# Layer 0's mixture of experts: the loop of extra blocks before the last block's outputs

## The chip, the cores and the metric

The kernel runs on one core of one Trainium2 chip. The metric is the device time of one execution in microseconds (us), as a median over runs. One execution is also recorded by the hardware profiler; all rows below come from that one. Engines are named as the profile names them: PE is TensorE, DVE is VectorE, ACT is ScalarE, POOL is GpSimd, and SP issues most of the DMAs.

## The reference, cut to what matters

The reference is a two-layer backbone over 256 context and 256 latent tokens, 1024 channels wide. Each layer mixes tokens (three branches) and then runs a mixture of experts. The change lies at the end of layer 0's mixture of experts and at the start of layer 1:

```python
combine = sum(one_hot(e_idx, 16) * w[..., None], axis=1)   # the two chosen experts of each token
gate = einsum('nd,edf->nef', t, w_gate)
up   = einsum('nd,edf->nef', t, w_up)
act  = silu(gate) * up * combine[..., None]
y    = einsum('nef,efd->nd', act, w_down)
...
xc = xc + mod_c[5] * f[:, :n_ctx]      # gated residual of the context tokens
xl = xl + mod_l[5] * f[:, n_ctx:]      # and of the latent ones
# the next layer begins with
hc = modulate(rms_norm(xc, norm_mix[1]), mod_c[0], mod_c[1])
hl = modulate(rms_norm(xl, norm_mix[1]), mod_l[0], mod_l[1])
```

## The kernel before, in words

The 512 tokens lie in four tiles of 128, `x[0]` to `x[3]`; tiles 0 and 1 are context, 2 and 3 latent. Layer 0's 16 experts are sorted by the number of their tokens and computed in blocks of 128 token slots. A block holds one large expert (`b < 5`, products split into three exact parts on PE) or two small ones of 64 slots (`b` from 5 on, computed half by half). `ORDER` fixes the row of blocks; the last two are block 4 (large) and block 8 (its halves are experts 12 and 13).

For every entry of that row `moe0` runs `full_in` or `half_in` (gate and up products), in the midst of it turns the entry before (`mid`), then runs the output products of the entry before (`finish`, with `down` or `outputs`). The outputs of ten blocks are written to a staging tensor `yd` in HBM. Those of the blocks in `KEPT` (4 and 8) stay on the chip as pairs `y`, already multiplied by the gate (`gated`).

When the row of blocks is through, three things follow:

- the staged rows of each token's two experts are gathered from `yd` by eight indirect DMAs on POOL (two for each token tile), and `total(t)` weights, adds and gates them and adds the sum to `x[t]`;
- a loop over extra blocks (`For_i`, `n` read from a register) covers experts with more tokens than their slots. Every engine and every DMA is waited for where the loop begins. In this run `n` is 0: the body's instructions do not show in the trace;
- `scatter` multiplies the kept pairs by one-hot matrices (`ot`) into rows of tokens, and `put2` adds them to `x`. `norm_r` then squares and sums `x[t]`, and `next_h` turns each tile for layer 1: `dr` (a diagonal of the norm), eight products on PE (L481), `hf` (scale and shift, DVE and ACT by turns), `hh` (ACT) and `hl` (DVE or POOL). Layer 1's first projection (L153 to L155) reads `hh` and `hl`.

The order on an engine is the scheduler's, except where `in_order(engine)` ties the instructions to the order in which they are written; before, this holds for PE through the row of blocks. `issue_after` puts single operations behind a named instruction. SP loads the weights in written order; `load_ahead` issues layer 1's first ones (`wq` twice, `wkv`) ahead.

Names that the text below uses: gates `gate[b]` (L1706, L1707), `total` (L1725 to L1728), the loop (L1742), the outputs of block 8 (L1470), `scatter` (L1524, L1525), `put2` (L1579), the squares (L346), `rv` and `rr` (L162, L163), `dr` (L476), `hf` (L486 on ACT, L488 on DVE), `hh` (L491), `hl` (L492), the splits `wh`, `wl` of a weight (L172, L173).

## Time and profile before

| | us |
|---|---|
| median of 3 runs | 1539.14 (1538.92 to 1540.22) |
| profiled execution, its own time | 1538.08 |
| profiled execution, span from first to last instruction | 1536.0 |
| PE busy | 1416.1 (92%) |
| DVE busy | 932.9 (61%) |
| ACT busy | 669.9 (44%) |
| POOL busy | 116.2 (8%) |

PE is busy nearly everywhere; what it is not busy with stands in a few holes. The change concerns the stretch from about 885 to 970 us. Times are counted from the span's start.

### The profile page before, as it was taken

How to read it: one execution, taken by the hardware profiler on the slowest of the kernel's cores; microseconds unless marked ns; L12 is line 12 of the kernel's file. 1: busy time of each engine (PE TensorE's matmuls, PEld its weight loads, DVE VectorE, ACT ScalarE, POOL GpSimd, SP SyncE). 2: the span in 40 equal slices, each digit the busy share in tenths (PEclk: the TensorE clock that was granted, in tenths of full speed). 3: DMA queues.
4: the chain of work that ended last, by engine and by line, in shares of the span. 5: the costliest groups of instructions: out<-in, count | busy, mean ns of one | idle time of the engine just before them, and what ended most of it. 6: DMA issues, size and time to landing. Idle time of an engine off the chain costs nothing. (4 is left out here: it accounts for less than half of the span.)

```text
span 1536.0 us, 20642 instructions
## 1 busy us (share of the span) xinstructions
PE 1416.1 (92%) x7431; PEld 929.2 (60%) x7431; DVE 932.9 (61%) x2154; ACT 669.9 (44%) x1333; POOL 116.2 (8%) x127
## 2 busy tenths in 40 slices
PE   5989999999999998699999966899999997999996
PEld 3766665687675666565555635788788775333332
DVE  4575556866564278897554666757977786423322
ACT  3344445735343235364454624555775553211112
POOL 1110000010000003200000022300001000000000
PEclk9999999999999999899999987999999999999999
DMA  8535425421135884499999993332333268899994
GB/s 324 208 144 217 152 96 199 144 101 57 56 108 205 310 299 145 170 354 381 421 421 422 418 362 130 139 136 87 120 128 100 97 223 348 364 423 424 424 423 178
DMA packets 56777, 363.11 MB, mean 236 GB/s; under 512 B 6368, under 2 KB 6368, under 8 KB 18528
## 3 DMA queue, kind: packets, MB, share of 16 engines
q1 hardware_dynamic: 47376, 328.49, 54.7%
q0 software_dynamic: 6400, 23.08, 4.4%
q10 hardware_dynamic: 2896, 10.19, 1.7%
q8 instruction: 60, 0.98, 0.3%
q14 instruction: 45, 0.37, 0.1%
HBM read 350.19 MB, written 11.54 MB: 236 GB/s over the span
## 5 line engine op out<-in xcount | busy, mean ns | idle before, releaser
L173 DVE TENSOR_TENSOR wl<-w,wh 128x512 fp32r<-128x512 f32 (+2 forms) x456 | 311.1, 699 | 184.2 <-ACT wh L172 168.2
L172 ACT CAST wh<-w 128x512 fp32r<-128x512 f32 (+2 forms) x456 | 270.8, 607 | 259.7 <-PE acc L233 127.3
L232 PE MATMUL acc<-hh,wh 128*128 128x512 f32 (+1 forms) x528 | 183.9, 348 | 0.2 <-ACT wh L172 0.2
L234 PE MATMUL acc<-hh,wl 128*128 128x512 f32 (+1 forms) x528 | 179.9, 341 | 1.4 <-DVE wl L173 1.4
L233 PE MATMUL acc<-hl,wh 128*128 128x512 f32 (+1 forms) x528 | 180.6, 342 | 0.0
L1447 PE MATMUL at<-w,xT 128*64 128x512 f32 x512 | 122.0, 600 | 1.1 <-DVE act L1452 0.8
L232 PEld LDWEIGHTS acc<-hh,wh 128*128 128x128 f32 x528 | 100.1, 190 | 31.2 <-issue 10.8
L234 PEld LDWEIGHTS acc<-hh,wl 128*128 128x128 f32 x528 | 100.1, 190 | 14.6 <-DVE wl L173 3.1
L233 PEld LDWEIGHTS acc<-hl,wh 128*128 128x128 f32 x528 | 100.1, 190 | 11.9 <-issue 2.1
L154 PE MATMUL acc<-wl,hh 128*128 128x512 f32 (+3 forms) x256 | 90.5, 354 | 5.4 <-DVE wl L173 5.4
L153 PE MATMUL acc<-wh,hh 128*128 128x512 f32 (+3 forms) x256 | 90.4, 356 | 2.8 <-DVE rv L162 2.3
L155 PE MATMUL acc<-wh,hl 128*128 128x512 f32 (+3 forms) x256 | 88.8, 350 | 0.0
L515 ACT ACTIVATE p<-at,nm 128x512 f32<-128x512 f32 (+1 forms) x96 | 59.1, 617 | 45.7 <-DVE nm L514 45.2
L1447 PE MATMUL acc<-w,xT 128*64 128x512 f32 x320 | 76.7, 606 | 1.6 <-DMA w<-in_moeu_dram 1.6
L163 POOL TENSOR_TENSOR rr<-rv,mhalf 128x1 f32<-128x1 f32 (+2 forms) x41 | 33.3, 813 | 524.5 <-DVE rv L162 517.0
L1447 PEld LDWEIGHTS at<-w,xT 128*64 128x64 f32 x512 | 33.5, 136 | 59.5 <-issue 55.2
L514 DVE TENSOR_REDUCE nm<-at 128x1 f32<-128x512 f32 (+1 forms) x96 | 56.5, 594 | 12.5 <-PE at L628 7.7
L232 PE MATMUL acc<-oh,wh 128*128 128x512 f32 (+1 forms) x160 | 59.5, 373 | 0.0
L154 PEld LDWEIGHTS acc<-wl,hh 128*128 128x128 f32 x256 | 49.7, 194 | 11.8 <-DVE wl L173 7.6
L1470 PE MATMUL at<-w,aT 128*64 128x512 f32 x256 | 56.7, 595 | 0.0
L233 PE MATMUL acc<-ol,wh 128*128 128x512 f32 (+1 forms) x160 | 55.9, 350 | 0.0
L234 PE MATMUL acc<-oh,wl 128*128 128x512 f32 (+1 forms) x160 | 55.8, 349 | 0.0
(504 smaller groups left out, 2638.8 us busy)
## 6 DMA issues: line engine op xcount, KB each, us to landing
w<-in_moeg_dram SPq DMA_DIRECT2D x64, 1024.0 KB, 16.0
w<-in_moeu_dram SPq DMA_DIRECT2D x64, 1024.0 KB, 17.9
w<-in_moed_dram SPq DMA_DIRECT2D x64, 1024.0 KB, 18.9
w<-in_wmod_dram SPq DMA_DIRECT2D x48, 1024.0 KB, 5.3
w<-in_wg_dram SPq DMA_DIRECT2D x24, 1024.0 KB, 4.8
w<-in_wb_dram SPq DMA_DIRECT2D x12, 1024.0 KB, 4.7
w<-in_wout_dram SPq DMA_DIRECT2D x8, 1024.0 KB, 7.1
w<-in_wx_dram SPq DMA_DIRECT2D x4, 1024.0 KB, 5.0
```

The lines of the kernel that those rows point to most:

```text
L153: nc.tensor.matmul(acc, ah, bh, start=start, stop=False)
L154: nc.tensor.matmul(acc, ah, bl, start=False, stop=False)
L155: nc.tensor.matmul(acc, al, bh, start=False, stop=stop)
L172: nc.scalar.copy(h, src)
L173: nc.vector.tensor_sub(l, src, h.bitcast(F32))
L232: nc.tensor.matmul(a[:, :n], h[:, i, :], hh[:, k, t0:], start=k == 0, stop=False)
L233: nc.tensor.matmul(a[:, :n], h[:, i, :], hl[:, k, t0:], start=False, stop=False)
L234: nc.tensor.matmul(a[:, :n], l[:, i, :], hh[:, k, t0:], start=False, stop=k == kc - 1)
L514: nc.vector.tensor_reduce(nm, sc[h][:, :nk], axis=AX.X, op=OP.max, negate=True)
L515: nc.scalar.activation(p[:, :nk], sc[h][:, :nk], AF.Exp, bias=nm, accum_out=sm)
L1447: nc.tensor.matmul(a[i * 64:i * 64 + 64], xT[:, k], ws[i][k // 4][:, k % 4], start=k == 0, stop=k == 7, tile_position=(0, i * 64))
L1470: self.nc.tensor.matmul(ya[n][64 * j:64 * j + 64], aT[:, k, 64 * j:64 * j + 64], w[k // 2][:, k % 2, n * 512:(n + 1) * 512], start=k == 0, ...
```

## The change

The loop of extra blocks now stands ahead of the turn and the output products of block 8's second half. The gathers of tiles 2 and 3 go into the buffers of the inputs `xh` and `xl`, and are issued when block 4's outputs begin; those of tiles 0 and 1 go into weight buffers, after the last weight loads. `total(2)` and `total(3)` precede the loop, `total(0)` runs beside the last outputs, and `total(1)`, wholly on DVE, in the midst of `scatter`. `scatter` goes through all four tiles of one half of the channels, then of the other; the squares are taken by halves. After the loop, until layer 1's tokens are turned, PE and DVE each follow the written order. The gates are computed one block earlier. Inside the loop's body buffers change too; the body isn't run here.

```diff
     def load_ahead(self, *loads):
-        ready = [self.load(*a) for a in loads]
-        self.ready.extend(ready)
+        ready, self.ready = self.ready, ()
+        loaded = [self.load(*a) for a in loads]
+        self.ready = collections.deque([*ready, *loaded])
...
-        for t in (2, 3, 0, 1):
-            for n in range(2):
+        for n in range(2):
+            for t in (2, 3, 0, 1):
                 a = bank()
...
             def put2(t, n, a):
                 c = x[t][:, n * 512:(n + 1) * 512]
-                ins = nc.vector.tensor_add(c, c, a)
-                if (t, n) == (3, 1):
-                    for i in (0, 1):
-                        total(i, (self.last, ins))
+                nc.vector.tensor_add(c, c, a)
+                if n == 0:
+                    sq[t] = self.small.tile([128, 2], F32, name="ssq")
+                    if t == 1:
+                        total(1)
+                if t == 1:
+                    if n:
+                        self.norms[t] = self.norm_r(x[t], junk)
+                    return
+                nc.scalar.activation(junk[:, :512], c, AF.Square, accum_out=sq[t][:, n:n + 1])
                 if n:
-                    self.norms[t] = self.norm_r(x[t], junk)
+                    ss = self.small.tile([128, 1], F32, name="ss")
+                    nc.vector.tensor_add(ss, sq[t][:, 0:1], sq[t][:, 1:2])
+                    self.norms[t] = self.rstd(ss, 1, D)
...
+            def rows(t, y):
+                ys[t] = y
+                for i in range(2):
+                    nc.gpsimd.indirect_dma_start(out=y[i], out_offset=None, in_=self.yd,
+                                                 in_offset=bass.IndirectOffsetOnAxis(ap=rt["row"][:, i, t:t + 1], axis=0))
+            def total(t):
+                y1, y2 = ys[t]
+                nc.scalar.activation(y1, y1, AF.Copy, scale=rt["w1"][:, t])
+                nc.vector.scalar_tensor_tensor(y1, y2, rt["w2"][:, t], y1, op0=OP.mult, op1=OP.add)
+                nc.vector.tensor_tensor(y1, y1, g2[t // 2], op=OP.mult)
+                nc.vector.tensor_tensor(x[t], x[t], y1, op=OP.add)
...
-                    with self.tc.issue_after(self.made[1].ins):
+                    with self.tc.issue_after(cut.ins):
                         for i, q in enumerate(KEPT):
...
+                    for t in (2, 3):
+                        rows(t, [T.tile([128, 8, 128], F32R, name=s).bitcast(F32).rearrange("p k q -> p (k q)")
+                                 for s in ("xh", "xl")])
                 if before:
                     finish(*before[:3])
+                    cut = self.cut
...
+            for t in (0, 1):
+                w = w2.tile([128, WG], F32, name="w")
+                rows(t, [w[:, i * D:(i + 1) * D] for i in range(2)])
-            turn(*before[:2], before[3])
             for t in (2, 3):
-                total(t, (self.made[0], self.made[-1]))
-            finish(*before[:3])
+                with self.tc.issue_after(gated[0].ins), self.tc.issue_after(gated[1].ins):
+                    total(t)
             order.close()
-            ot = T2.tile([128, 8, 128], F32R, name="xT", bufs=1)
-            last = [y + (self.spread(ot[:, 4 * i:4 * i + 4], rt["tok"][:, i]),) for i, y in enumerate(kept)]
-            self.load_ahead(*((self.I["wq"][1, i], 4) for i in range(2)), (self.I["wkv"][1], 8))
+            self.load_ahead(*((self.I["wq"][1, i], 4) for i in range(2)))
...
             with self.tc.For_i(0, n, 1) as i:
...
+            self.order = ExitStack()
+            for g in (mybir.EngineType.PE, mybir.EngineType.DVE):
+                self.order.enter_context(self.in_order(g))
+            turn(*before[:2], before[3])
+            ot = T2.tile([128, 8, 128], F32R, name="xT", bufs=1)
             junk = T2.tile([128, D], F32, name="yg", bufs=1)
-            self.feed(0, self.scatter(last, put2, self.acc))
+            spread = [self.spread(ot[:, 4 * i:4 * i + 4], rt["tok"][:, i]) for i in range(2)]
+            total(0)
+            finish(*before[:3])
+            self.load_ahead((self.I["wkv"][1], 8))
+            self.feed(0, self.scatter([y + (s,) for y, s in zip(kept, spread)], put2, self.acc))
             self.drain()
...
                     self.next_h(T, x[t], t, 1, hh, hl)
+            self.order.close()
             return mix, hh, hl, pre
```

In the rows of instructions below, line numbers after the change are the changed kernel's own. PE at the loop, before: `w,xT` are block 8's gate and up products, `tp<-cp,act` its turn, `w,aT` its outputs, and the compare and branch is the loop's beginning.

```order
L1447 MATMUL acc<-w,xT 64x512 x8
L1460 MATMUL tp<-cp,act 128x64 x4
L1470 MATMUL acc<-w,aT 64x512 x16
L1741 TENSOR_LOAD rctl
L1742 COMPARE_AND_BRANCH
```

PE where it leaves the loop, after the change (`yh,xT` and so on are `scatter`'s products):

```order
L1756 COMPARE_AND_BRANCH
L1756 UNCONDITIONAL_BRANCH
L1463 MATMUL tp<-cp,act 128x64 x4
L1473 MATMUL acc<-w,aT 64x512 x16
L1527 MATMUL acc<-yh,xT 128x512
L1528 MATMUL acc<-yl,xT 128x512
```

The second turn and the sixteen output products moved from ahead of the loop to behind it.

DVE between `scatter`'s sums and the first `dr`, before (numbers are those of the buffers; `x2`, `x3`, `x0`, `x1` are the token tiles):

```order
L1579 TENSOR_TENSOR x2_4997<-x2_4997,acc_8585 128x512
L1579 TENSOR_TENSOR x3_4998<-x3_4998,acc_8597 128x512
L1579 TENSOR_TENSOR x3_4998<-x3_4998,acc_8603 128x512
L162 TENSOR_SCALAR rv_8593<-ss_8591 128x1
L173 TENSOR_TENSOR wl_8729<-w_8219,wh_8728 128x512
L173 TENSOR_TENSOR wl_8733<-w_8219,wh_8732 128x512
L1726 SCALAR_TENSOR_TENSOR w_8169<-w_8169,rw2_5014 128x1024
L1726 SCALAR_TENSOR_TENSOR w_8172<-w_8172,rw2_5014 128x1024
L1727 TENSOR_TENSOR w_8169<-w_8169,xg_8021 128x1024
L162 TENSOR_SCALAR rv_8619<-ss_8617 128x1
L476 TENSOR_SCALAR dr_8673<-cp_72,rr_8594 128x128
```

The same after the change, from the first tile's second half on:

```order
L1585 TENSOR_TENSOR x2_4997<-x2_4997,acc_8619 128x512
L1598 TENSOR_TENSOR ss_8626<-ssq_8590 128x1
L163 TENSOR_SCALAR rv_8628<-ss_8626 128x1
L1585 TENSOR_TENSOR x3_4998<-x3_4998,acc_8632 128x512
L1598 TENSOR_TENSOR ss_8639<-ssq_8598 128x1
L163 TENSOR_SCALAR rv_8641<-ss_8639 128x1
L1585 TENSOR_TENSOR x0_4995<-x0_4995,acc_8645 128x512
L1598 TENSOR_TENSOR ss_8652<-ssq_8606 128x1
L163 TENSOR_SCALAR rv_8654<-ss_8652 128x1
L1585 TENSOR_TENSOR x1_4996<-x1_4996,acc_8658 128x512
L163 TENSOR_SCALAR rv_8666<-ss_8664 128x1
L477 TENSOR_SCALAR dr_8684<-cp_72,rr_8629 128x128
```

The first `dr` moved behind the sums and norms of all four tiles, and each `ss` reads squares of its own tile that ACT takes in between.

DVE from the turn of the first tile to that of the third after the change (`hf`, `hl` of tile 2, then `dr`, `hf`, `hl` of tile 3, then the splits `wl` of layer 1's first weights); before, both `dr` and all of these splits stood ahead of the first `hl`:

```order
L489 TENSOR_SCALAR hf_8686<-tp_8696,modA1_2512,modB1_2513 128x128
L493 TENSOR_TENSOR hl_8679<-hf_8686,hh_8678 128x8x128
L477 TENSOR_SCALAR dr_8708<-cp_72,rr_8642 128x128
L489 TENSOR_SCALAR hf_8710<-tp_8711,modA1_2512,modB1_2513 128x128 x2
L489 TENSOR_SCALAR hf_8710<-tp_8720,modA1_2512,modB1_2513 128x128 x2
L493 TENSOR_TENSOR hl_8679<-hf_8710,hh_8678 128x8x128
L174 TENSOR_TENSOR wl_8732<-w_8185,wh_8731 128x512
L174 TENSOR_TENSOR wl_8736<-w_8185,wh_8735 128x512
```

The second tile's `dr` moved behind the first tile's `hl`, and the splits behind the second tile's.

## Rows read from the trace of the kernel before

**Rows 1.** Stretches by their busy time; columns in the first row.
```profile
core 0: us, PE busy (x) PEld busy (x) DVE busy (x) ACT busy (x) POOL busy (x), PEclk, DMA share, GB/s
885.90:908.50 22.60, 18.10 (x77) 8.76 (x77) 12.35 (x23) 4.99 (x8) 4.39 (x4) 0.92 1.01 419
925.90:935.40 9.50, 9.48 (x32) 7.31 (x32) 7.03 (x11) 5.94 (x10) 0.95 (x1) 0.79 0.67 231
951.20:967.30 16.10, 16.07 (x83) 13.54 (x83) 11.60 (x29) 11.02 (x22) 3.27 (x2) 0.92 0.07 19
```
**Rows 2.** Timeline at the loop: start, us, engine, line, instruction, [idle before, releaser].
```profile
903.98 0.43 PE L1460 MATMUL tp<-cp,act 64*128 64x64 f32 x4 [1.61 <-DVE act L1452]
904.34 7.81 PE L1470 MATMUL acc<-w,aT 128*64 128x512 f32 x32
...
917.95 0.94 POOL L1718 DMA_INDIRECT w<-yd,rrow  x1 [0.30 <-issue]
925.87 0.80 PE L1524 MATMUL acc<-yh,xT 128*128 128x512 f32 x1 [13.72 <-issue]
```
**Rows 3.** The gather issued at 917.95 alone, and SP's waits, 905 to 930.
```profile
DMA to landing us min/median/max: 6.4/6.4/6.4
...
SPq L1742 <- DMA w<-yd,rrow: 10.7, 2, 8.4
```
**Rows 4.** DMA queues, 885.9 to 924.4: packets, MB, share of 16 engines.
```profile
q1 hardware_dynamic: 1247, 9.01, 57.6%
q0 software_dynamic: 1152, 4.19, 29.3%
```
**Rows 5.** The same, 904 to 906, gathers beside weight loads.
```profile
q0 software_dynamic: 125, 0.48, 59.9%
q1 hardware_dynamic: 48, 0.35, 42.4%
```
**Rows 6.** PE's wait behind the gates of the kept blocks.
```profile
892.60 0.80 PE L154 MATMUL acc<-wl,ah 128*128 128x512 f32 x1 [2.89 <-DVE wl L173]
```
**Rows 7.** Timeline from the first tile's norm to layer 1's first product.
```profile
936.15 3.25 POOL L1727 TENSOR_TENSOR w<-w,xg 128x1024 f32<-128x1024 f32 x1 [2.64 <-DVE w L1726]
937.19 2.30 DVE L476 TENSOR_SCALAR dr<-cp,rr 128x128 f32<-128x128 f32 x1
939.54 3.23 PE L481 MATMUL tp<-dr,x 128*128 128x128 f32 x16 [4.15 <-DVE dr L476]
951.21 0.77 PE L153 MATMUL acc<-wh,hh 128*128 128x512 f32 x1
```
**Rows 8.** Groups by shape, 905 to 919.6: count | busy us, mean ns.
```profile
L1726 DVE SCALAR_TENSOR_TENSOR w<-w,rw 128x1024 f32<-128x1024 f32 x2 | 2.6, 1280 | 4.3 <-ACT w L1725 4.3
L1507 DVE SCALAR_TENSOR_TENSOR act<-acc,rws,w 128x512 f32<-128x512 f32 x2 | 1.4, 742 | 0.0
```
**Rows 9.** Groups by shape, 939.5 to 957.
```profile
L488 DVE TENSOR_SCALAR hf<-tp,modA,modB 128x128 f32<-128x128 f32 x11 | 4.2, 404 | 3.1 <-PE tp L481 2.6 <-ACT hf L486 0.5
L486 ACT ACTIVATE hf<-tp,modB,modA 128x128 f32<-128x128 f32 x9 | 3.9, 451 | 2.8 <-DVE hf L488 2.8
L1579 DVE TENSOR_TENSOR x<-x,acc 128x512 f32<-128x512 f32 x4 | 2.5, 682 | 2.2 <-POOL x L1728 2.2
L492 DVE TENSOR_TENSOR hl<-hf,hh 128x1024 fp32r<-128x1024 f32 x2 | 2.4, 1216 | 0.0
L346 ACT ACTIVATE yg<-x 128x1024 f32<-128x1024 f32 x2 | 2.1, 1049 | 10.2 <-DVE x L1579 10.2
L491 ACT CAST hh<-hf 128x1024 fp32r<-128x1024 f32 x2 | 2.1, 1044 | 0.1
L476 DVE TENSOR_SCALAR dr<-cp,rr 128x128 f32<-128x128 f32 x3 | 0.8, 279 | 0.1
```

**Rows 10.** The page's costliest groups: the split's cast and difference (512 columns).
```profile
L173 DVE TENSOR_TENSOR wl<-w,wh 128x512 fp32r<-128x512 f32 (+2 forms) x456 | 311.1, 699 | 184.2 <-ACT wh L172 168.2
L172 ACT CAST wh<-w 128x512 fp32r<-128x512 f32 (+2 forms) x456 | 270.8, 607 | 259.7 <-PE acc L233 127.3
```

More of the change, by code (lines that the diff above doesn't have):

```diff
@@ L172, in split @@
         nc.scalar.copy(h, src)
-        nc.vector.tensor_sub(l, src, h.bitcast(F32))
+        self.cut = nc.vector.tensor_sub(l, src, h.bitcast(F32))
         return h, l
@@ L1385, in full_turned, with full_in @@
         return xh, xl
-    def full_in(self, T, x, ws, acc, mid=None, late=None):
+    def full_in(self, T, x, ws, acc, mid=None, late=None, act=None):
         nc = self.nc
@@ L1399, in full_in @@
                 self.fill()
-        act = T.tile([128, 512], F32, name="act", bufs=3)
+        if act is None:
+            act = T.tile([128, 512], F32, name="act", bufs=3)
         nc.scalar.activation(act, ga, AF.Silu)
@@ L1569, in pair, with middle @@
                 return tuple(T.tile([128, 2, 512], F32R, name=n, bufs=b) for n, b in (h, l))
+            def middle():
+                return T.tile([128, 4, 128], F32R, name="ot", bufs=1).bitcast(F32).rearrange("p k q -> p (k q)")
             def put1(t, n, a):
                 c = slice(n * 512, (n + 1) * 512)
-                z = T.tile([128, 512], F32, name="act", bufs=3)
+                z = middle()
                 nc.vector.tensor_mul(z, a, g2[t // 2][:, c])
@@ L1591, in out @@
                     i = len(kept)
-                    if i:
-                        w = wa.tile([128, WG], F32, name="w").bitcast(F32R).rearrange("p (a n c) -> p a n c", a=2, n=2)
-                        y = w[:, 0], w[:, 1]
-                    else:
-                        y = pair(("yh", 1), ("yl", 1))
+                    y = pair(("xh", 2), ("xl", 2)) if i else pair(("yh", 1), ("yl", 1))
                     kept.append(y)
@@ L1668, in finish @@
                 out(self.down(T, mids[b], downs[p], self.acc) if b < 5 else
-                    self.outputs(mids[b], [downs[q] for q in MADE[b]], self.acc), b)
+                    self.outputs(mids[b], [downs[q] for q in MADE[b]], self.acc, b in KEPT), b)
+            def rows(t, y):
[9 more added lines that the diff above has]
+                nc.vector.tensor_tensor(x[t], x[t], y1, op=OP.add)
+            ys, sq = {}, {}
             fetch(todo[0][1])
@@ L1707, in moe0 @@
                             nc.vector.scalar_tensor_tensor(gate[q], g2[1], fl[:, 1:2], gate[q], op0=OP.mult, op1=OP.add)
+                    for t in (2, 3):
+                        rows(t, [T.tile([128, 8, 128], F32R, name=s).bitcast(F32).rearrange("p k q -> p (k q)")
+                                 for s in ("xh", "xl")])
                 if before:
                     finish(*before[:3])
+                    cut = self.cut
                 before = p, b, b < 5 or not first, act
             weights(before[1])
-            ys = {t: [] for t in (2, 3, 0, 1)}
@@ L1714, in moe0 @@
-            for t in ys:
-                w = wa.tile([128, WG], F32, name="w")
-                for i in range(2):
-                    ys[t].append(w[:, i * D:(i + 1) * D])
-                    nc.gpsimd.indirect_dma_start(out=ys[t][i], out_offset=None, in_=self.yd,
-                                                 in_offset=bass.IndirectOffsetOnAxis(ap=rt["row"][:, i, t:t + 1], axis=0))
-            def total(t, after):
-                y1, y2 = ys[t]
-                eng = nc.gpsimd if t == 1 else nc.vector
-                with self.tc.issue_after(after[0].ins), self.tc.issue_after(after[1].ins):
-                    nc.scalar.activation(y1, y1, AF.Copy, scale=rt["w1"][:, t])
-                    nc.vector.scalar_tensor_tensor(y1, y2, rt["w2"][:, t], y1, op0=OP.mult, op1=OP.add)
-                    eng.tensor_tensor(y1, y1, g2[t // 2], op=OP.mult)
-                    eng.tensor_tensor(x[t], x[t], y1, op=OP.add)
@@ L1743, in moe0 @@
                 ex = nc.values_load(ctl[0:1, ds(i + 1, 1)], engines=eng, min_val=0, max_val=NE - 1)
-                wx = self.expert_at(0, ex)
+                wx = self.expert_at(0, ex, self.NAMES[:2])
                 rc, wc = self.extra(X, rt, cnt, rt["we"])
```

14 lines of the change are left out of this document (9 added, 5 removed).

## Prediction

> **What bounds the kernel now.** I read the stretch busy times first, then the timeline around the loop, then the DMA queues, then the groups by shape. PE bounds the program nearly everywhere. It works in the 16.1 us of layer 1's first projection without a hole [rows 1], and what the change can win or lose is holes of PE between 885 and that projection.
>
> The largest hole is the loop's. PE ends the last outputs at 904.34 + 7.81 = 912.15 and starts `scatter` at 925.87, after 13.72 us of waiting [rows 2]. What ends it is the last gather: issued at 917.95, landed 6.4 us later, so at 924.35 [rows 2, 3]. SP waited 8.4 us for just these gathers where the loop begins [rows 3]. From landing to PE's first product pass 925.87 - 924.35 = 1.5 us.
>
> Under the gathers lies a full DMA. From 885.9 to 908.5 the 16 engines are busy without pause (share 1.01) at 419 GB/s [rows 1]. From 885.9 until the last landing at 924.4, 38.5 us, the weight queue takes 57.6% of the engines' time for 9.01 MB, which is 22.2 us, and the gathers take 29.3% for 4.19 MB, which is 11.3 us [rows 4].
>
> The second place is the chain from `scatter` to layer 1. `scatter` ends at about 935.4, the first tile's `dr` ends at 939.49, its turn starts at 939.54, and layer 1's first product runs at 951.21 [rows 1, 7].
>
> **The change part by part.** I follow the time at which layer 1's projection runs on without holes: 951.2 before.
>
> *When the loop lets go.* The gathers no longer wait for the last block, but the engines of the DMA were full then already. What must have landed at the loop is what had to before, less the load of `wkv`, which now follows it (1.05 MB; at 9.01 MB in 22.2 us, that is 2.6 us). So 22.2 - 2.6 + 11.3 = 30.9 us of full engines from 885.9: 916.8. For engines that end unevenly I take 918. The other candidate is DVE. In ACT's queue the scaling of tile 0's rows stands ahead of those of tiles 2 and 3, so DVE's sums wait for the fifth gather. If the gathers have half of the engines' time, the fifth has its bytes after 5/8 x 22.6 = 14 us, and lands near 904. From there: 1.2 for the scaling, 1.3 for the kept pair (cast and difference of 512 columns [rows 10]), two `total` of 1.28 + 1.22 + 1.22 = 3.7 each (1.28 [rows 8], 1.22 as `hl` of the same size [rows 9]), about 1.2 for `aT` and block 8's last gate product: 915, just under 918. So PE goes on at 918 + 1.5 = 919.5, which is 6.4 earlier than 925.87.
>
> *What now follows the loop.* Four turns of 0.43, a copy on DVE, sixteen output products of 7.81 us [rows 2]; before, these stood ahead of the loop, beside the gathers. PE has then waited some 20 us and starts at the lower clock. Before, `scatter` came out of its wait so: 9.5 us at a granted clock of 0.79 lose 0.21 x 9.5 = 2.0 us [rows 1]. Here 1.3 us of that falls on the turn and the copy, so I take 1.3 + 7.8 + 1.4 = 10.5 us. `scatter` begins at 930.0, or 4.1 later than before. `total(0)` and the one-hot products lie beside these outputs and cost nothing; were they late, they would cost up to their 5.1 us.
>
> *From `scatter` to the first turn.* DVE now goes in written order, so everything here adds up. The second half of the kept pair: 0.74 + 0.61 + 0.70 = 2.1, until 932.1 [rows 8, 10]. Four sums of 0.68 [rows 9]: 934.8. `total(1)`: 3.7, so 938.5. Then for each of tiles 2, 3, 0: a sum 0.68, a square over half a row on ACT, the read of its sum, `ss`, `rv`. A full square takes 1.05 [rows 9]; for the half one with its read I estimate 0.8, for the small ones and the handing over 0.3: 1.8 each, 943.9. Tile 1: 0.68 + 1.05 + 0.6 = 2.3, 946.2. `dr` 0.28 [rows 9]: the first turn starts at 946.6. Before, it started at 939.54, because DVE put the first `dr` ahead of the other tiles' sums. PE is idle from about 937.
>
> *The turns.* The first turn takes 3.23 us at the low clock [rows 7], half of it before the first `hf` can start: 1.6. Then `hf` by turns on DVE and ACT, four pairs of 0.40 + 0.45 [rows 9] with handing over 3.6, `hh` 1.04: 952.8. Now `hl` 1.22 and only then the second tile's `dr` 0.28: 954.4. Again 1.6 + 3.6 + 1.04: 960.7. Then `hl` 1.22 and the first `wl` 0.70: 962.7 [rows 10]. Until then PE can run two products of the projection. Before, the second tile's turn followed the first at once and the splits were ready.
>
> *The rest.* 962.7 - 951.2 = 11.5 us later. The projection starts at the low clock, as before (0.08 x 16.1 = 1.3 us lost [rows 1]), but after a longer pause: 1 more. The two early products give back 0.5. Sum: 12.0 us slower.
>
> *Edits with no price.* The gates leave the place where they held PE for 2.9 us [rows 6]; PE comes to the loop earlier by that and waits there, so nothing is gained as long as the DMA decides. The loads of `wkv` and the second of `wx` go later by some 15 and 30 us; the projection's 16 us and the products after it cover them, and if not, a load of 6 us would show. The loop's body doesn't run.
>
> The trace has one row where DVE and POOL meet: the first `dr` took 2.30 us, from 937.19 to 939.49, while POOL multiplied from 936.15 to 939.40 [rows 7]; the three others took 0.28 [rows 9]. The Trainium skill (SBUF — State Buffer, "Who interferes with whom") says that VectorE and GpSimd share one pair of ports as an exclusive lock, and that the later one is blocked until the first is done. The trace agrees: 2.30 us ended with POOL's 3.25. By that rule the first `dr` costs 0.28 now that POOL's two operations are gone, which I took; without it, 2.0 us more.
>
> The unknowns by bounds: the release between 916.8 (queues perfectly packed) and 924.4 (as before); the chain of squares between 1.2 and 2.3 a tile, which is 3 us; `hf` between 0.45 a step on each engine side by side (2.0 us a tile) and 4.0. That the release and the chain err together I allow for with -8 and +6 us.
>
> **The rivals.**
>
> *A, as worked out:* the written order on DVE gives back more than the earlier release. 1538.08 + 12.0 = 1550.1 by the profiled execution's own time; the runs' median stands 1.1 above it, so 1551. Own range 1547 to 1556.
>
> *B, a shorter tail:* the release comes at 917 and handing over costs less, squares 1.2 a tile and `hf` 2.0: 1 + 2 + 3 = 6 us off, 1545. For it speaks that the scheduler of before left 4.15 us in the same place too [rows 7]; against it, that each `ss` stands behind its own square in DVE's queue.
>
> *C, faster:* the loop does not wait for the `wq` loads, and its end is set by DVE and the gathers. Taken at its best, gathers alone on the engines, the release is 912; PE goes on at 913.5, `scatter` at 924.0. If the tail then takes the 25.3 us that it took before (951.2 - 925.9) and `scatter` runs at full clock (2 less), the projection runs from 947.3: 3.9 earlier, 1535. It decides from a release before 914 and a tail under 25 us; either one alone doesn't. Against it: SP's wait covers all queues, and the tail's order is written.
>
> *D, later still:* the gathers get less than half of the engines' time. In 904 to 906 both queues have work: 125 gather packets take 59.9% and 48 weight packets 42.4% of 32 engine-us, so 0.15 and 0.28 us each [rows 5]. Taken one for one, gathers would have 0.15 / 0.43 = 35%; the fifth has its bytes after 5/8 x 11.3 / 0.35 = 20 us, near 910, and DVE comes to the loop at 921 or 922. With the seventh gather behind it the release is some 924, which costs 6 us: 1557. The measured 125 to 48 speaks against one for one. The Trainium skill (DMA: Bandwidth & Descriptors, "Queues, rings and completion order") says that each DMA engine takes turns among its queues, packet by packet; by that rule the time would be that of D.
>
> **How the numbers follow.** A 0.64 (1551), B 0.16 (1545), C 0.08 (1535), D 0.08 (1557), and 0.04 for a shift that ends within 0.2% either way. 0.2%, about 3.1 us, is what a measurement of this kernel can tell from no change. Faster: C, 0.08. Same: 0.04, and 0.02 out of B, 0.06. Slower: the rest, 0.86. The range 1543 to 1557 holds A, most of B and half of D, about 0.82.
>
> **What would show it.** Right: a hole of some 20 us on PE at the loop that ends near 919.5; outputs of block 8 behind it; the first turn some 16 us after `scatter` begins; the second tile's `dr` behind the first's `hl`; the projection without holes from about 963. DVE and PE stand idle by turns between 937 and 963. Wrong: a release near 912, a first turn within 10 us of `scatter`'s begin, or a projection that starts before 952.

## The result, and the profile after the change

The changed kernel takes 1556.18 us (median of 4 runs, 1555.08 to 1562.84), the kernel before 1539.68 beside it: a ratio over the runs of 1.0122 with a 95% interval of 1.0107 to 1.0137 (the two medians alone make 1.0107). That is slower, as predicted. The median lies at the upper end of the range, 0.8 us inside it, 5.2 us above the predicted 1551 and 0.8 under rival D's 1557; the ratio times the 1539.14 of the kernel before, as the prediction had it, makes 1557.9, just outside. Of all runs here and below one came out slow, at 2034.19 us in e5, and its ratio is without it.

The page's first lines. Against before, the span is 18.0 us longer.

```profile
span 1554.0 us, 20648 instructions
...
PE 1423.9 (92%) x7431; PEld 933.8 (60%) x7431; DVE 933.0 (60%) x2159; ACT 672.5 (43%) x1339; POOL 108.4 (7%) x125
```

Not all of the 18 us arise at the change. TensorE's instructions up to block 8 are the same, in the same order, yet the same product is already 4.2 us late at 885 (L1412 starts at 884.61 instead of 880.42; both are matched by name and place in the two timelines). 2.9 of it arise in one place, 16 us from the start. Timelines of PE, of before and then of the changed kernel (start, us, engine, line, instruction, count):

```profile
15.93 1.92 PE L394 MATMUL tp<-w,csil 128*32 128x512 f32 x16
```
```profile
16.26 3.64 PE L395 MATMUL tp<-w,csil 128*32 128x512 f32 x16
```

The sixteen products take 1.92 us in one execution and 3.64 in the other, and what waits for them keeps the difference. Another 1.5 us come between 605 and 660. Stretch 614 to 620, before and after (columns as in [rows 1]):

```profile
614.00:620.00 6.00, 6.00 (x24) 4.86 (x24) 4.37 (x20) 2.61 (x6) 0.00 (x0) 0.84 0.47 168
```
```profile
614.00:620.00 6.00, 5.16 (x21) 4.52 (x22) 3.74 (x14) 3.28 (x8) 0.00 (x0) 0.63 0.86 313
```

There the granted clock was 0.63 instead of 0.84. In the first place the clock's column reads 1.00 in both, so it doesn't show the cause; but there too each product takes about twice as long (0.12 and 0.23 us), as between the two levels of the clock elsewhere (behind the loop 0.23 and 0.43 us from one product of 512 columns to the next), so the clock is likely. In twelve further kernels, whose beginning was not touched, the same product at 885 came 0.2 to 7.5 us late. So I take this head from every profiled execution: what is "late" below is the start of a product at 1014 (L233) less the head at 885. By that the change costs 17.25 - 4.19 = 13.06 us.

Now the loop, in PE's timeline; it answers to [rows 2]:

```profile
898.25 3.65 PE L1450 MATMUL acc<-w,xT 128*64 128x512 f32 x16
927.14 0.69 PE L1463 MATMUL tp<-cp,act 64*128 64x64 f32 x4 [25.23 <-DVEq L1756]
927.76 9.95 PE L1473 MATMUL acc<-w,aT 128*64 128x512 f32 x32
937.64 0.50 PE L1527 MATMUL acc<-yh,xT 128*128 128x512 f32 x1
```

PE waits 25.23 us, and the row names DVE's queue at the loop (L1756), not a transfer. DVE's own timeline says what it did before it came to the loop, and ACT's why it began so late:

```profile
894.50 0.62 ACT L1511 CAST yh<-act 128x512 fp32r<-128x512 f32 x1 [2.21 <-DVE act L1510]
915.81 1.15 ACT L1691 ACTIVATE w<-w,rw 128x1024 f32<-128x1024 f32 x1 [20.70 <-DMA w<-yd,rrow]
916.87 0.60 ACT L1511 CAST yh<-act 128x512 fp32r<-128x512 f32 x1
917.38 2.18 ACT L1691 ACTIVATE xh<-xh,rw 128x1024 f32<-128x1024 f32 x2
```
```profile
917.50 0.69 DVE L1511 TENSOR_TENSOR yl<-act,yh 128x512 fp32r<-128x512 f32 x1 [21.66 <-ACT yh L1511]
918.55 2.48 DVE L1692 SCALAR_TENSOR_TENSOR xh<-xl,rw,xh 128x1024 f32<-128x1024 f32 x2 [0.36 <-ACT xh L1691]
920.95 2.35 DVE L1693 TENSOR_TENSOR xh<-xh,xg 128x1024 f32<-128x1024 f32 x2
923.22 2.35 DVE L1694 TENSOR_TENSOR x<-x,xh 128x1024 f32<-128x1024 f32 x2
925.49 0.42 DVE L1464 COPY aT<-tp 128x256 f32<-128x256 f32 x1
925.94 0.69 DVE L1455 TENSOR_TENSOR act<-act,acc 64x512 f32<-64x512 f32 x1
```

ACT stands 20.70 us at the scaling of tile 0's rows (the fifth gather). A cast and two scalings whose data are there stand behind it in ACT's order, and DVE waits 21.66 us for the cast. Then DVE works almost without a pause to 926.6. The last gather had landed at 921.5 (issued at 899.7, 21.8 us on its way, by the view of the gathers' line):

```profile
L1686 POOL DMA_INDIRECT w<-yd,rrow x4: 933/935/937, 896.0 to 899.7; - x4
...
DMA to landing us min/median/max: 8.7/18.6/21.8
```

How the two queues shared the engines while both had work, 904 to 912; the columns are those of [rows 4], and it answers to [rows 5]:

```profile
q1 hardware_dynamic: 304, 2.21, 66.6%
q0 software_dynamic: 302, 1.11, 34.6%
```

302 gather packets to 304 others, and 34.6% of the engines' time for the gathers.

Behind the loop, the tail to layer 1's projection answers to [rows 7] (PE, and DVE's first diagonal):

```profile
953.39 0.28 DVE L477 TENSOR_SCALAR dr<-cp,rr 128x128 f32<-128x128 f32 x1
```
```profile
953.72 3.79 PE L482 MATMUL tp<-dr,x 128*128 128x128 f32 x16 [8.37 <-DVE zxp L638]
960.51 0.79 PE L154 MATMUL acc<-wh,hh 128*128 128x512 f32 x1 [3.01 <-ACT hh L492]
961.97 3.78 PE L482 MATMUL tp<-dr,x 128*128 128x128 f32 x16 [0.67 <-DVE dr L477]
968.76 0.79 PE L154 MATMUL acc<-wh,hh 128*128 128x512 f32 x1 [3.01 <-ACT hh L492]
970.62 0.79 PE L155 MATMUL acc<-wl,hh 128*128 128x512 f32 x1 [1.07 <-DVE wl L174]
```

The projection runs on from 970.62 instead of 951.2: 19.4 later, 15.2 without the head.

### The profile page after: what moved, and what is told of

Read it like the earlier page. It is cut to its first block, busy times and chain, and to the rows that moved or that the text cites. A ratio compares the mean times of both kernels' runs of the same rounds, so it can differ in the third digit from the quotient of the medians.

```text
span 1554.0 us, 20648 instructions
## 1 busy us (share of the span) xinstructions
PE 1423.9 (92%) x7431; PEld 933.8 (60%) x7431; DVE 933.0 (60%) x2159; ACT 672.5 (43%) x1339; POOL 108.4 (7%) x125
## 5 line engine op out<-in xcount | busy, mean ns | idle before, releaser
L173 ACT CAST wh<-w 128x512 fp32r<-128x512 f32 (+2 forms) x456 | 270.9, 607 | 263.5 <-PE acc L234 132.1
L233 PE MATMUL acc<-hh,wh 128*128 128x512 f32 (+1 forms) x528 | 183.9, 348 | 0.2 <-ACT wh L173 0.2
L233 PEld LDWEIGHTS acc<-hh,wh 128*128 128x128 f32 x528 | 100.0, 189 | 31.1 <-issue 10.8
L233 PE MATMUL acc<-oh,wh 128*128 128x512 f32 (+1 forms) x160 | 59.5, 373 | 0.0
L154 PEld LDWEIGHTS acc<-wh,hh 128*128 128x128 f32 x256 | 49.5, 194 | 15.7 <-ACT hh L492 6.6
```

Source lines behind the costliest of these rows:

```text
L154: nc.tensor.matmul(acc, ah, bh, start=start, stop=False)
L173: nc.scalar.copy(h, src)
L233: nc.tensor.matmul(a[:, :n], h[:, i, :], hh[:, k, t0:], start=k == 0, stop=False)
```

## The experiments

All are timed against the kernel before on the same chip (its median was 1538.5 to 1538.9 in these). "Late" is the measure explained above, from the one profiled execution of each. It has noise of its own: e8 is 2.9 us later than the changed kernel by it, and not slower in the median.

```
kernel           built on   late at 1014     median us   ratio to before [95%]
changed kernel   -           17.25-4.19= 13.06  1556.18  1.0122 [1.0107, 1.0137]
e8_gates_back    changed     19.79-3.86= 15.93  1555.26  1.0107 [1.0090, 1.0124]
e9_wq_late       changed     13.80-1.79= 12.01  1551.79  1.0086 [1.0069, 1.0103]
e1_order         changed      8.15-0.23=  7.92  1550.6   1.0078 [1.0062, 1.0095]
e4_last          changed      4.43-1.16=  3.27  1544.03  1.0035 [1.0024, 1.0046]
e7_tail          e1           4.19-7.54= -3.35  1538.23  0.9996 [0.9985, 1.0007]
b6_loop_first    e7          -2.55-5.77= -8.32  1532.01  0.9954 [0.9939, 0.9970]
e6_buffers       before       3.17-3.71= -0.54  1539.45  1.0005 [0.9995, 1.0015]
e5_gates         before      -5.25-1.36= -6.61  1533.63  0.9966 [0.9954, 0.9978]
b3_sums          e5          -0.80-1.94= -2.74  1535.6   0.9977 [0.9964, 0.9989]
b4_late_loads    b3          -8.07-1.77= -9.84  1527.42  0.9923 [0.9901, 0.9944]
b5_rest_behind   b4          -8.61-0.69= -9.30  1529.82  0.9951 [0.9934, 0.9967]
b1_rework        changed      -3.77-2.06= -5.83  1533.63  0.9965 [0.9955, 0.9975]
```

**e1: ScalarE's order at the loop.** Is it the order of ACT, or the transfers, that holds the loop?

```diff
-                nc.scalar.activation(y1, y1, AF.Copy, scale=rt["w1"][:, t])
+                if t < 2:
+                    with self.tc.issue_after(self.made[0].ins):   # behind block 8's silu
+                        nc.scalar.activation(y1, y1, AF.Copy, scale=rt["w1"][:, t])
+                else:
+                    nc.scalar.activation(y1, y1, AF.Copy, scale=rt["w1"][:, t])
```

> Changed kernel, with the two scalings of tiles 0 and 1 (ScalarE) queued behind block 8's last silu, so that the second cast of block 4's kept output and the scalings of tiles 2 and 3 no longer stand behind the fifth gather. Theory (a head-of-line wait on ScalarE): VectorE, idle until 917.5 in the changed kernel, takes its split at about 895 and its totals as the first four gathers land (899.5 to 912.0); its last operation ahead of the loop ends near 917 instead of 926.6. The loop is then released by the last gather's landing (921.5) and TensorE goes on near 922.5 instead of 927.1: 4.6 us less, about 1551.5 us. Rival (the drain of the transfers, or of the loop's own branches, sets the release whatever VectorE does): TensorE still goes on near 927, 1556 us. Of the 2.9 us that the changed kernel lost in its first 31 us: if they belong to the program, they are here too; if to one execution, they need not be.

1550.6 us, 5.1 us less late. ACT now scales tile 2's rows first, and DVE finishes its totals before the last gathers are there; in PE's timeline the loop ends at 918.42:

```profile
918.42 0.69 PE L1463 MATMUL tp<-cp,act 64*128 64x64 f32 x4 [20.48 <-issue]
919.04 9.59 PE L1473 MATMUL acc<-w,aT 128*64 128x512 f32 x32
```

Without the head of 0.23 that is 918.2, instead of 922.95. So some 5 us of the slowdown were ACT's head of the line, and with DVE out of the way the transfers release PE about where the prediction had put it (919.5).

**e9: the loads of `wq` behind the loop.** The changed kernel, with a one-element copy by DVE into each buffer behind the loop, so that the load follows it:

```diff
-            self.load_ahead(*((self.I["wq"][1, i], 4) for i in range(2)))
...
+            self.guard = x[2][0:1, 0:1]      # load() copies it into the buffer first
+            self.load_ahead(*((self.I["wq"][1, i], 4) for i in range(2)), (self.I["wkv"][1], 8))
+            self.guard = None
```

> The changed kernel with the two loads of wq held until the loop has been passed (a copy of one element into each buffer, which VectorE makes behind the last block's splits). Theory (gathers and loads take turns packet by packet, so 2.1 MB less beside the gathers brings them in 5 us earlier): the fifth gather's product starts on ScalarE 4 to 6 us sooner than the 915.8 of the changed kernel, the loop is left as much sooner, and the median is 1550 us (1548 to 1552). Rival 1 (the gathers have a share of their own that does not depend on how much is queued beside them, as the prediction had it): the fifth gather at the same time, median 1556. Rival 2 (wq now comes late for its splits): the gain is lost again in front of the projection, 1555 to 1560.

1551.79 us. The fifth gather is there sooner (ACT's timeline):

```profile
909.72 1.15 ACT L1694 ACTIVATE w<-w,rw 128x1024 f32<-128x1024 f32 x1 [17.00 <-DMA w<-yd,rrow]
```

That is 6.1 us sooner by the records, and 3.7 when both heads are taken off (907.9 and 911.6). So what is queued beside the gathers decides when they land, and rival 1, the prediction's fixed share, falls. Of the 3.7 us sooner that PE left the loop (921.04 - 1.79 = 919.25), only 1.05 are left at 1014. PE's wait for the split of `wq` grew only from 1.07 to 1.36 us, against rival 2; but then the clock came back late. Stretches of e9 and of the changed kernel, each from the projection's first free product to the clock's return (columns as in [rows 1]):

```profile
964.80:971.50 6.70, 6.67 (x26) 5.80 (x26) 3.08 (x6) 0.89 (x2) 0.00 (x0) 0.55 0.57 207
```
```profile
970.60:973.60 3.00, 2.98 (x7) 2.39 (x8) 2.19 (x5) 0.62 (x1) 0.00 (x0) 0.52 0.14 16
```

From there on the low level (0.63 us for a product of 512 columns, 0.39 at the high one) lasted 6.7 us in e9 and 3.0 in the changed kernel. In the 3.4 us ahead of it, with one product in them, the granted clock was 1.00 in e9 (960.6 to 964.0) and 0.50 in the changed kernel (966.6 to 970.0): in e9 it had come back and fell again. Why it did so in one and not in the other isn't settled.

**e8: the gates where they were.** Does TensorE's stall of [rows 6] matter in the changed kernel?

```diff
-                    with self.tc.issue_after(cut.ins):
+                    with self.tc.issue_after(self.made[1].ins):
```

> The changed kernel with one line as it was before it: the two gates' copies wait again for the second block's middle, not for the weight split just ahead of them. Theory (transfers and ScalarE's order decide when the loop is entered, so TensorE's 4.65 us by 896 lead to nothing): the gap of 2.9 us in front of block 8's products is back, the release of the loop moves by less than 1 us, and the median is 1556 us (1554 to 1558). Rival (the early gates are worth here what they were worth in the structure of before, where they alone gave 6.6 us beside the clock): 1561 to 1563.

1555.26 us against 1556.18: no change. The stall is back in PE's timeline, and the loop ends at 927.51 - 3.86 = 923.65, 0.7 later:

```profile
896.50 0.50 PE L155 MATMUL acc<-wl,ah 128*128 128x512 f32 x1 [2.93 <-DVE wl L174]
...
927.51 0.69 PE L1463 MATMUL tp<-cp,act 64*128 64x64 f32 x4 [22.72 <-DVEq L1756]
```

The other 2 us by which it is later at 1014 are the clock again, at its low level from 970.75 to 977.4. The median doesn't show them, and I don't count them.

**e5: the early gates alone, in the kernel before.** The same line, the other way round, in `before`:

```diff
...
-                    with self.tc.issue_after(self.made[1].ins):
+                    with self.tc.issue_after(cut.ins):
...
```

> The kernel before with one part of the change alone: the gates of the kept blocks computed one block earlier. Theory (an edit with no price: the 2.9 us that TensorE waits for at 892.6 go, and come back as a longer wait at the loop, which is released by the transfers): within 0.5 us of before, 1539.5 us. Rival (the stall is on the path): 2.9 us less, 1536.5 us.

1533.63 us: faster than before by 5 us. Here a part of the change that the prediction had priced at nothing is worth 6.6 us. The gathers of the later tiles in this structure wait for a free buffer. POOL's timeline with the fifth gather in e5; then, from before, DVE's with the sum of tile 2 and POOL's with the fifth gather:

```profile
904.97 0.94 POOL L1719 DMA_INDIRECT w<-yd,rrow  x1 [2.89 <-PE acc L1470]
```
```profile
911.90 1.22 DVE L1728 TENSOR_TENSOR x<-x,w 128x1024 f32<-128x1024 f32 x1
```
```profile
913.39 1.74 POOL L1718 DMA_INDIRECT w<-yd,rrow  x1 [8.02 <-SPq L1742]
```

In e5 it is PE's products that free the buffer. Before, the gather goes out 0.3 us behind the end of tile 2's total (913.12) and 1.2 behind PE's last output (912.15); its row names SP's queue, so that it waits for the buffer of tile 2's rows is read from the times, and from e6 below, where other buffers let it out sooner. So the line took the stall away and moved the buffers too; how much each of them gives isn't separated. The last gather in e5, in POOL's timeline; then PE's:

```profile
908.70 1.22 POOL L1719 DMA_INDIRECT w<-yd,rrow  x1 [0.30 <-issue]
```
```profile
922.49 0.80 PE L1524 MATMUL acc<-yh,xT 128*128 128x512 f32 x1 [13.63 <-issue]
```

The last gather goes out at 908.70 instead of 917.95 [rows 2]. It lands 12.3 us later, not 6.4, since it is no longer alone, and that is still 3.4 us earlier than before.

**e6: only the early gathers, in the kernel before.** Tiles 0 and 1 get buffers that are free sooner:

```diff
-                w = wa.tile([128, WG], F32, name="w")
+                w = (w2 if t < 2 else wa).tile([128, WG], F32, name="w")
...
```

> The kernel before, with nothing of the change but other buffers: the rows of tiles 0 and 1 are gathered into the second weight pool, so that they need not wait for the buffer of tile 2's rows. It asks why the early gates alone brought 5.2 us where they take away a wait of 2.9 us: in that run the fifth gather went out at 905.0 and the transfers had no hole, in the kernel before it went out at 913.4 and the transfers stood still for some 3 us around 911. Theory (half of the gain is the hole, which comes from a buffer that tile 2's total frees): gathers 5 to 8 go out right behind the first four, at 905 to 910, the last lands near 921, the loop is released near 922 instead of 925.4: 3.3 us less, 1535.6 us. Rival (the gates' wait alone moves everything behind it): release stays near 925, 1538.9 us.

1539.45 us, no change, a miss for my theory. All gathers are out by 906.5, but they crowd one another. ACT scales tile 2's first row at 914.06, or 910.4 without the head (907.28 before), the totals end later, and PE is now released by DVE's queue, as in the changed kernel:

```profile
914.06 1.15 ACT L1725 ACTIVATE w<-w,rw 128x1024 f32<-128x1024 f32 x1 [8.78 <-DMA w<-yd,rrow]
```
```profile
930.20 0.80 PE L1524 MATMUL acc<-yh,xT 128*128 128x512 f32 x1 [15.79 <-DVEq L1742]
```

**e4: the loop back in its place.** The changed kernel with the turn and block 8's outputs ahead of the loop again; early gathers, early gates and the written orders stay. Lines that are not shown give block 8's kept outputs a weight buffer, load `wkv` ahead of the loop again and hold the first `wx` behind it.

```diff
...
+            turn(*before[:2], before[3])
...
+            finish(*before[:3])
...
             with self.tc.For_i(0, n, 1) as i:
...
-            turn(*before[:2], before[3])
-            total(0)
-            finish(*before[:3])
```

> Changed kernel with the loop back behind block 8's outputs (its turn and outputs ahead of the totals of tiles 2 and 3, total of tile 0 ahead of the loop, kept output 8 in a weight buffer, the spread one-hots ahead of the loop, layer 1's first wx load held behind it), the rest as changed: early gathers, early gates, tile-inner scatter, squares by halves, the fixed orders. Theory (the loop's place costs the 10 us of outputs that it pushes behind the drain): outputs end near 917, the loop is released by the transfers at 924 to 925, the scatter starts near 925.5 instead of 937.6, the tail stays 33 us: projection without holes from 958.5 instead of 970.6, 1544 us. Rival (the place costs little, since the outputs now wait for totals and the totals for gathers): release near 930, 1549 us.

1544.03 us: 9.8 less late than the changed kernel, but still 3.3 later than before. The time was forecast (1544), the way to it was not: `scatter` begins at 922.34 instead of 925.5, and the first turn comes 18 us behind (940.33), against 16.1 in the changed kernel. What is left is the tail.

**e7: the tail as before, on e1.** Back to both halves of a tile at once, full squares, no written order behind the outputs, tile 1's two sums on POOL:

```diff
-        for n in range(2):
-            for t in (2, 3, 0, 1):
+        for t in (2, 3, 0, 1):
+            for n in range(2):
...
-                nc.scalar.activation(junk[:, :512], c, AF.Square, accum_out=sq[t][:, n:n + 1])
...
+                    self.norms[t] = self.norm_r(x[t], junk)
...
```

> The run with ScalarE's order mended (1550.6 us), with the tail behind the loop as in the kernel before: scatter with the tile outer, one square a tile, VectorE's and TensorE's order not fixed behind the outputs, tile 1's multiply and add on GpSimd. The loop's place, gathers and gates stay as changed. Theory (the fixed orders and the half-inner scatter make the tail: scatter to projection took 33.0 us with them and 25.3 us in the kernel before): 8 us less, 1542.6 us. Rival (the tail is long because TensorE comes out of a longer idle stretch, or because the outputs run in it): no more than 2 us less, 1549 us.

1538.23 us: level with before. The tail gives back 11.3 us (7.92 - (-3.35)): more than the 5.1 of ACT's order, and the largest of the steps. Which of its four edits gives how much isn't separated. The first turn comes 8.1 us behind `scatter`'s begin (936.85), not 16.1:

```profile
944.95 2.05 PE L482 MATMUL tp<-dr,x 128*128 128x128 f32 x16 [0.37 <-DVE dr L477]
```

**b6: e7 with `wq` and `wkv` behind the loop.** The guard of e9 on e7. Is the loop's place bad of itself?

```diff
...
+            self.guard = x[2][0:1, 0:1]
...
```

> The kernel of e7 (loop ahead of the last block's outputs, the scalings of tiles 0 and 1 behind block 8's silu on ScalarE, the tail as before the change) with wq and wkv held behind the loop. Theory (what is left of the loop's new place is the transfers that it has to wait for): e7's 1538.2 less some 7, as the same step gave between b3 and b4: 1531 us (1529 to 1533). Rival (the place of the loop costs of itself, since VectorE's totals stand ahead of its entry): 1537 to 1539, and then TensorE is released by VectorE's queue at the same time as in e7.

1532.01 us, 5.0 less late than e7: the loop ahead of the outputs, with ACT's order, the tail and the loads put right, is faster than before. It isn't shown to gain anything by its place: b4 below, with the loop where it was, is faster still (0.9923 of before against 0.9954).

**b3: each total behind its own tile's sums, on e5.**

```diff
-                if (t, n) == (3, 1):
-                    for i in (0, 1):
-                        total(i, (self.last, ins))
+                if n and t < 2:
+                    total(t, (self.last, ins))
...
```

> The kernel before with early gates (1533.6 us), and the totals of tiles 0 and 1 queued behind these tiles' own sums instead of ahead of them. In the early-gates run VectorE stood at tile 1's sums from 936.5 to 938.8, for GpSimd's add, and the first turn's results of 936.5 were taken out only at 941.2. Theory (that wait is on the path): the first results leave at about 937, and projection goes on without holes 4 us earlier: 1529.5 us. Rival (GpSimd's slow multiply and add now end later, and hold tile 1's norm): 1533 us or more.

1535.6 us, a miss: not better than e5 (1533.63). Tile 1's sums on POOL then end later (948.4 instead of 938.7).

**b4: late loads, on b3.** `wq`, `wkv` and `wx` behind the loop, held in the way of e9:

```diff
...
+                if (t, n) == (2, 0):
+                    self.guard = c[0:1, 0:1]
+                    self.load_ahead(*((self.I["wq"][1, i], 4) for i in range(2)), (self.I["wkv"][1], 8), (self.I["wx"][1, 0], 16))
+                    self.guard = None
...
```

> The run before in this list (totals behind sums, early gates), and layer 1's first loads (wq twice, wkv, wx) issued behind the loop instead of ahead of it. Theory (the loop waits for every transfer, and 3 MB of these are not needed until 20 us behind it): the last gather lands near 914 instead of 921, VectorE's splits of block 8 release the loop near 917.5 instead of 921.3: 3.5 us less again, 1526 us. Rival (the late weights hold the splits and with them the projection): no gain, 1529.5 us or more.

1527.42 us, the best here: 11.1 us faster than before (1538.53 on that chip) and some 29 faster than the changed kernel. PE waits 9.20 us at the loop instead of 13.72 [rows 2]:

```profile
918.49 0.80 PE L1528 MATMUL acc<-yh,xT 128*128 128x512 f32 x1 [9.20 <-issue]
```

**b5: a written order behind b4's loop.** Tiles 2 and 3 turned first, each diagonal a tile ahead, the totals of tiles 0 and 1 behind tile 3's turn:

```diff
...
+                self.next_h(T, x[2], 2, 1, hh, hl, functools.partial(diag, 3), functools.partial(split, 0))
+                self.next_h(T, x[3], 3, 1, hh, hl, none, functools.partial(split, 2))
+                self.rest(0)
...
```

> The kernel of b4 with a written order behind the loop: tiles 2 and 3 turned first, each diagonal made one tile early, the splits of wq between the casts, and the totals of tiles 0 and 1, all on VectorE, behind tile 3's low half. Theory (in b4 the first turn waits for a diagonal that VectorE makes behind the totals): 1523 us (1521 to 1525). Rival (the late totals hold tiles 0 and 1's turns, and the projection of those tiles waits): 1527 us or more.

1529.82 us: the rival. The first turn is earlier (927.43 against 931.91 in b4), but PE then stops for tiles 0 and 1 and for layer 1's normalised queries, three waits of 1.8 to 3.0 us. From 944 to 1000 it waits 10.0 us, and 6.3 in b4: the 3.4 that the earlier turn had gained, without the heads, are gone.

```profile
963.84 0.58 PE L159 MATMUL acc<-wh,hl 128*128 128x256 f32 x1 [1.82 <-POOL hl L498]
...
976.08 0.30 PE L593 MATMUL tp<-cp,qn 128*128 128x128 f32 x1 [1.82 <-DVE qn L586]
979.40 0.66 PE L593 MATMUL tp<-cp,qn 128*128 128x128 f32 x2 [3.01 <-DVE qn L586]
```

**b1: several parts at once.** The loop in its old place, all totals ahead of it, late loads, early gates and gathers, a written tail that goes tile by tile with each diagonal one tile early.

```diff
-                if (t, n) == (3, 1):
-                    for i in (0, 1):
-                        total(i, (self.last, ins))
...
+            for t in (0, 1):                             # ahead of the loop
+                with self.tc.issue_after(gated[0].ins), self.tc.issue_after(gated[1].ins):
+                    total(t)
...
-        dr = hp.tile([128, 128], F32, name="dr", bufs=2)
-        nc.vector.tensor_scalar(dr, self.ident, self.norms[t][:, 0:1], None, op0=OP.mult)
+        dr = self.drs.pop(t)                         # made during the tile before
```

> A version meant to beat both. From the changed kernel: early gathers and early gates stay; the loop stands behind block 8's outputs and behind all four totals; layer 1's first loads (wq, wkv, wx) are issued behind the loop; scatter with the tile outer; one square a tile, with the reciprocal root one tile later; each tile's diagonal made while the tile before is turned. Theory: transfers are through by 917, VectorE's last total ends near 924 and releases the loop at 924 to 926 (925.4 before); no total stands behind the loop, so the first turn comes right behind the scatter, 9 us behind the release (14 before), and projection goes on without holes near 946 (951.2 before): 1534 us. Rival (VectorE's splits and evacuations bound the tail anyway, and the weights loaded late hold the projection): 951 or later, 1539 us or more.

1533.63 us, as expected (1534); but the early gates alone (e5) have the same median on the same chip. A written order need not be slow: here the first turn comes 10.3 us behind `scatter` (926.83 to 937.13), against 16.1 in the changed kernel and 13.7 before. That it is so because the diagonal isn't behind the next tiles' squares is argued, not tried alone.

## Why the prediction was right and wrong

*The sign was right, and for the reason given:* the tail loses more than the release brings. The table gives the account, in steps of lateness from before: the early gates -6.6 (e5); the loop's place with the early gathers +3.3 (from e5 to e7); the tail +11.3 (from e7 to e1); ACT's order +5.1 (from e1 to the changed kernel); sum 13.1. By the medians the same steps are -5.2, +4.6, +12.4 and +5.6, sum 17.3. The tail is the largest in both; each step holds for the structure in which it was tried. The prediction put the first at nothing, and the last too, since it had DVE at the loop at 915.

*The failed step* is "If the gathers have half of the engines' time, the fifth has its bytes after 5/8 x 22.6 = 14 us, and lands near 904", and with it "915, just under 918". The fifth landed at 915.8, 911.6 without the head; from there to DVE's end it took 10.8 us, as predicted (11), so DVE was through at 926.6, or 922.4, and the loop was left at 922.95 and not at 919.5. That is +3.4. Rival D's mechanism came true: the fifth gather near 910, DVE at the loop at 921 or 922, and I had given it 0.08. Its price didn't: it said 6 us for a later release, and 3.4 were measured. That the median comes within 1 us of D's 1557 is luck; the head and the rest (below) fill the gap.

I had read 125 to 48 packets [rows 5] as evidence against turns one for one. But in those 2 us the weight queue was running out, so that they show no share between two full queues. The next 2 us of the kernel before, 906 to 908, in the same view; from 908 to 910 the weight queue moves nothing:

```profile
q0 software_dynamic: 177, 0.63, 78.6%
q1 hardware_dynamic: 31, 0.17, 20.9%
```

The changed kernel ends its loads in the same way: 155 gather packets to 42 others from 916 to 918. While both had work, over 8 us, it was 302 to 304, and the share 34.6%, against D's 35%. The Trainium skill (DMA: Bandwidth & Descriptors, "Queues, rings and completion order") says that a DMA engine takes turns among its queues packet by packet; the trace agrees, if what the profile counts as a packet is what the Trainium skill calls one, which no run here shows. Since a gather packet takes half as long as a weight packet (0.15 and 0.28 us), equal turns are a third of the time.

*The transfers' end was right.* 918 predicted; the last gather landed at 921.5, or 917.3 without the head. In e1, where DVE no longer decides, PE goes on at 918.2.

*From the loop on, the chain held term by term.* Release to `scatter` 10.5 (predicted 10.5), `scatter` to the first turn 16.1 (16.6), from there to the projection 16.9 (16.1): 43.5 against 43.2. The squares took 1.8 us a tile as estimated, PE stood idle, and the second diagonal followed the first `hl`, as the signs at the end of the prediction had it. Each turn took 2.1 us to its first `hf` instead of 1.6; that makes the last part longer. `dr` took 0.28 us at once; where POOL works beside it again, it doesn't (DVE in e7, then POOL):

```profile
944.61 0.28 DVE L477 TENSOR_SCALAR dr<-cp,rr 128x128 f32<-128x128 f32 x1
947.66 2.36 DVE L477 TENSOR_SCALAR dr<-cp,rr 128x128 f32<-128x128 f32 x1 [2.01 <-POOL rr L164]
```
```profile
947.60 2.33 POOL L1690 TENSOR_TENSOR x<-x,w 128x1024 f32<-128x1024 f32 x1
```

That is the 2 us of the prediction's "without it". The trace of before has more than the "one row where DVE and POOL meet": a split (L173) at 962.00 took 2.08 us instead of 0.69 while POOL made `hl` from 961.12 to 963.53.

*The rest was off by 2.6.* I had added 0.5 us behind the projection's start; 2.1 were given back by 1014 (15.2 late at the start, 13.06 there). The 1 us for the clock after "a longer pause" has nothing in the runs: from the free products on it was granted at 0.52 over 3.0 us, against 0.60 over 3.3 before (951.2 to 954.5). Some 1.1 are back early, most of it by the two early products: at 969 in before's time the same product is 14.1 late. The last 1.1 come at a later pause that both kernels have: before, PE came out of it with a granted clock of 0.74 (973.9 to 986.8), and in the changed kernel with 0.87 (992.2 to 1005.0). That is luck, and so is it that 12.0 and 13.06 lie so close: +3.7 and -2.6 nearly cancel.

*"Edits with no price" was right only here.* "Nothing is gained as long as the DMA decides" held in the changed kernel (e8). In the kernel before, the later gathers wait for buffers, and the same line is worth 6.6 us (e5): there the transfer that decided was itself issued late, and in e5 the fifth gather goes out 8.4 us sooner. [Rows 2 and 3] had a sign of it: the last gather issued 5.8 us behind PE's last output, and alone on the engines.

*What the sum makes of the 5.2 us:* +3.4 release, +0.3 tail, -2.6 rest, +4.2 head make 5.3. The head is shown for the profiled execution only. Whether every run of the changed kernel has it is open: e8 and e9, the same kernel but for one edit, had heads of 3.9 and 1.8, and the runs of before lay between 1535.5 and 1542.7. The profiled execution of before had the earliest head of all fourteen kernels, and yet it is only 0.8 us faster than its kernel's usual 1538.9. So it stays open what makes the last 4 us between the 13.1 of the steps and the 17.3 of the medians.

*Rivals B and C:* C's condition failed in both halves, the release near 914 and the tail under 25 us. Both come near in b6 (the loop is left at 920.09 - 5.77 = 914.3; the first turn, 938.13, comes 8.5 us behind `scatter`'s begin), and then the kernel is faster, as C said. B's short squares (1.2) didn't come.

## What to carry to other kernels

Where many loads and gathers are queued together, count packets: take the share of a queue from a long stretch in which both have work and neither runs out, and move what isn't urgent (here 2 MB of `wq`) behind the point that waits. Before a barrier, read each engine's queue in its own order: one operation that waits for a late transfer holds the ready ones behind it, and with them another engine's whole chain. And before a stall is priced at nothing because a transfer decides, ask why that transfer was issued when it was.

## What the runs showed of the hardware

- The same instructions up to 885 us, in 14 kernels: their profiled executions differ by up to 7.5 us there, and the sixteen products at 16 us took 1.92 or 3.64. An effect of 3 us can't be read from two spans alone.
- From the same product on, TensorE stayed at the low level for 3.0 us (changed kernel) or 6.7 (e8, e9); in the 3.4 us ahead the granted clock was 0.50 in the first and 1.00 in the other two.
- Two queues with work took turns one for one: 302 packets to 304 in 8 us. As one of them ran out, the counts of 2 us were 125 to 48 and 177 to 31.
- Issuing a gather earlier into full queues brings a part of it: in the changed kernel the eighth was issued 18.2 us earlier than before (899.7 against 917.95) and landed 2.9 earlier, or 22.4 and 7.0 without the head, its way having grown from 6.4 to 21.8.
